# Pre-norm weights as columns at the eviction of transposed activations, in a two-layer encoder on one core

## The chip, the cores and the metric

The kernel runs on one core of a Trainium2 chip. The core has engines with instruction streams of their own: TensorE (PE in the profile, its weight loads PEld), VectorE (DVE), ScalarE (ACT), GpSimd (POOL) and SyncE (SP), which here issues nearly all DMAs. Data lies in SBUF on 128 partitions; TensorE writes to the 8 banks of PSUM. What counts is the time of one launch on the device in microseconds (us), lower being better.

## The reference

An encoder of two layers works on x of 256 tokens by 1024 channels in float32. Each layer is a block of three token mixers with gates and then an MLP, both with a norm ahead of them (pre) and one behind them (post):

```python
def rmsnorm(x, g):
    return x * lax.rsqrt(jnp.mean(x * x, axis=-1, keepdims=True) + EPS) * g

for l in range(2):
    h = rmsnorm(x, g_mix_pre[l])
    z = h @ w_in[l] + b_in[l]                     # 1024 -> 5648
    y_m = mlstm_branch(...) @ w_up_mlstm[l]       # convolution, two directions, chunks of 128
    y_f = fourier_branch(...) @ w_up_fourier[l]   # 2-D Fourier mixing
    y_s = s5_branch(...)                          # two-way diagonal state space, gelu, GLU
    gates = sigmoid(z[..., OFF_GATE:]).reshape(..., 3, 1024)
    mixed = gates[0] * y_m + gates[1] * y_f + gates[2] * y_s
    x = x + rmsnorm(mixed @ w_out[l], g_mix_post[l])
    h = rmsnorm(x, g_ffn_pre[l])
    f = square(relu(h @ w_ffn1[l])) @ w_ffn2[l]   # 1024 -> 4096 -> 1024
    x = x + rmsnorm(f, g_ffn_post[l])
```

## The kernel before

**Products.** Every large product is made of three of TensorE, in a type of fewer bits: high part by high part, high by low, low by high (`mm3`, L259). So each piece of weights (512 KB as a rule) comes by a DMA of SP into a raw buffer, ACT copies it to the high part (L200) and DVE subtracts that from it for the low part (L202, `wload`). There are three raw buffers and four of each part; some pieces take slots of the two rings A and B instead. The normalised activations lie transposed, channels on partitions, as a high and a low part, `hT`.

**Pre-norm** (`prenorm`, L349). It works on one half of the tokens, 128 rows, at a time. First, ACT squares and sums the rows in two halves of 512 channels (L353), and POOL makes a root column of the sums in two steps (L338, L340). Second, DVE multiplies each half by the root column and by the weight vector, which a DMA has broadcast to all partitions, in one instruction with two tensors (L359). Third, TensorE transposes four blocks of 128 channels of a half into one PSUM bank (L186); ACT evicts the bank into the high part (L368) with a constant factor and DVE makes the low part (L369). One instruction of each evicts 512 columns.

**Order.** A planner fixes the order of each engine's list ahead of the run. It takes what is emitted first, first, unless its own reckoning says that something later can go sooner; a load that waits for a buffer, for example, lets later loads pass. At the three joints, where one block's last products meet the next block's pre-norm and first weights, the order of ACT and DVE is written out by hand instead (`meet`, L395, with the strings of `MEET`, L58): `0` and `1` are the next stage of the norms of the first and second half of the tokens (`norms`, L371: squares of the sum, then its addition to x together with the squares of the pre-norm, then scaling, then transposes with their eviction), `h` and `l` are the high and low part of one of the next block's weights, `P` stands for the products of the second half.

**Weight vectors of the norms.** `load_gains` (L414) broadcasts the post-norm's and the next pre-norm's vector, 512 KB each, into one slot of ring A, with one weight load between them.

**Columns.** `load_columns` (L459) loads small vectors, among them biases, as 108 rows of 128, transposes them once and keeps them as columns, one element to a partition; `col` picks one.

**Start.** SP's list begins with a 128x128 unit matrix (the first columns of `cst`), three small loads of the S5 parameters (`s5_columns`, L493, some sixty small DVE instructions follow on them), the two halves of the first 128 rows of x, the broadcast pre-norm weights, the other 128 rows of x, and the first projection's weights: three pieces (gates of the mLSTM and Fourier input) and then four of v. Then come the rest of `cst`, eight loads of S5 tables with short rows (L586, L591), biases and columns. TensorE makes the first projections of the first half of the tokens and then of the second (`tokens`, L264).

Of the kernel before, what the change touches and what calls it, by code (L numbers as in the profile page):

```python
# [15 lines left out]
P = 128  # L16
D = 1024
# [31 lines left out]
# weights of the products that end a block held in place of the ring's pieces  # L49
TAIL = 4  # L50
# amount of work on the side for a pair of channel tiles: in the mixers of a layer, in its MLP from a pair on
# [3 lines left out]
# parts that the mLSTM with the Fourier mixing and the S5 have in that work  # L55
MIX_SHARE = ((2.0, 1.0), (1.0, 2.0))
# ends of the blocks: stages of the two norms (0, 1), of the next weights' high and low parts (h, l), the products (P)
# [23 lines left out]
def shape_constants():  # L81
# [16 lines left out]
    for g in range(2):  # L98
# [10 lines left out]
        ("bg", 16), ("s5d", 2)]  # L109
# [9 lines left out]
def encoder_kernel(ctx: ExitStack, tc: tile.TileContext, a: dict, out: bass.AP):  # L119
# [68 lines left out]
    def wload(pieces, shape, in_ring=None):  # L188
        """a piece of weights in two parts, in three stages: its loading, one of ACT and one of DVE"""
# [17 lines left out]
    def after_weights(l):  # L207
        """what DVE is to begin no sooner than the weights already asked for, in a later layer"""
        return tc.issue_after(latest[0]) if l > 0 else ExitStack()
# [4 lines left out]
    def now(gen):  # L214
        """all stages of gen; what it returns"""
        while True:
            try:
                next(gen)
            except StopIteration as e:
                return e.value  # L220

    class Feed:
        """the first weights of a block, stage by stage; each piece goes to the end of its list"""
# [40 lines left out]
    def tokens(t, parts, together):  # L264
        """rows t of the normalised activations times the weights of parts: what to do with the products, the number
        of columns, units, rows of tiles in a unit. The first half of the tokens comes when the weights do: the
        products that need their high parts alone go first"""
# [32 lines left out]
    def tick(budget):  # L300
        """let the work beside the main stream of products go on by about that amount"""
# [10 lines left out]
    def flush(which=None):  # L312
        """finish the work of one thread (or of both), the other going on beside it"""
# [7 lines left out]
    def wstat_pair(w, c0, nk, ahi, alo, kper=4, budget=0.0):  # L321
        """two [128 channels, 256 tokens] products of w[:, c0:c0+256]^T with the transposed activations, in one bank:
        its first product alone clears what the bank knows of what is written"""
# [11 lines left out]
    def rstd_of(ss):  # L335
        """(sum of squares / D + EPS)^-0.5 / sqrt(D) as a [128,1] column"""
# [12 lines left out]
    def prenorm(t, g):  # L349
        """rows t of x normalised, split and transposed into hT, in three stages"""  # L350
# [5 lines left out]
        hs = []  # L356
        for c in range(2):
            h = w2k()
            stt(h, x_sb[:, t, half(c)], rs, g[:, half(c)], ALU.mult, ALU.mult)  # L359
            hs.append(h)  # L360
        yield
        for c in range(2):
# [3 lines left out]
            o = [hT[i][:, c * 4:(c + 1) * 4, t * P:(t + 1) * P] for i in range(2)]  # L366
            p3 = ps.rearrange("p (k q) -> p k q", k=4)
            act(o[0], p3, AF.Copy, scale=ROOT_D)  # L368
            stt(o[1], p3, ROOT_D, o[0].bitcast(F32), ALU.mult, ALU.subtract)  # L369

    def norms(t, ps, gpost, gpre):  # L371
        """rows t of x take the sum of a block, normalised; then their normalisation for the next; four stages"""
# [18 lines left out]
    def ordered():  # L391
        """ACT and DVE take what is emitted here in this order"""
        return tc.manual_schedule(engines={mybir.EngineType.Activation, mybir.EngineType.DVE})

    def meet(products, chain0, chain1, feed, order):  # L395
        """the end of a block: the second half of the tokens' products beside the norms of the first half, the next
# [919 lines left out]
```

## Time and profile before

| what | value |
|---|---|
| three runs | 842.96, 845.17, 845.23 us; median 845.17 |
| span of the profiled execution, first to last instruction | 842.6 us |
| TensorE busy | 816.7 us (97%) |
| DVE busy | 605.7 us (72%) |
| ACT busy | 467.0 us (55%) |
| POOL busy | 29.3 us (3%) |
| moved by DMA | 146.32 MB, 174 GB/s on average |

The page gives no time of its own for the profiled execution beside the span, so the span is set against the three runs. A row of a timeline has the start in us from the span's start, the time in us from the group's first start to its last end, the engine, the line, the operation, what it writes and reads, how many instructions are merged in it, and in brackets how long the engine had been idle before and what ended that. Neighbouring instructions of one engine overlap a little, so the sum of durations can be more than the stretch that they fill.

### The profile page before, as it was taken

What the parts mean: (1) busy time and instruction counts of PE and PEld (TensorE: products, weight loads), DVE (VectorE), ACT (ScalarE), POOL (GpSimd) and SP (SyncE); (2) the same over time, 40 slices, a digit from 0 to 9 for tenths busy, and PEclk for the clock granted to TensorE, in tenths of its full rate; (3) what the DMA queues carried; (4) which work ended last, traced back from release to release, by engine and by line L of the source; (5) the groups of instructions that cost most, each with busy time, mean ns of one, the idle gap of its engine ahead of it and who ended that gap; (6) DMA issues with size and microseconds to landing.
All of it is one profiled execution on the core that took longest, in us unless ns stands there. A gap on an engine that the chain in (4) does not pass through costs nothing.

```text
span 842.6 us, 15382 instructions
## 1 busy us (share of the span) xinstructions
PE 816.7 (97%) x6077; PEld 757.2 (90%) x6077; DVE 605.7 (72%) x1087; ACT 467.0 (55%) x770; POOL 29.3 (3%) x50
## 2 busy tenths in 40 slices
PE   4999999999999999999989999999999999999997
PEld 3799999999878999999878999999997799999995
DVE  6798999787585576677477899787866845555554
ACT  4567844685464447567554444567655644444452
POOL 1000100010020000000010010000000100000000
PEclk9999999999999999999999999999999999999999
DMA  6775734446755665756656562454666556566571
GB/s 191 220 187 166 206 103 138 126 129 205 233 181 166 188 193 142 236 168 196 200 166 181 148 194 80 129 173 150 184 193 225 173 160 192 182 194 182 193 225 50
DMA packets 116965, 146.32 MB, mean 174 GB/s; under 512 B 17909, under 2 KB 98973, under 8 KB 116637
## 3 DMA queue, kind: packets, MB, share of 16 engines
q1 hardware_dynamic: 116892, 145.35, 57.7%
q8 instruction: 47, 0.77, 0.4%
q14 instruction: 26, 0.21, 0.1%
HBM read 143.80 MB, written 1.52 MB: 172 GB/s over the span
## 4 chain that ended last, share of the span: by engine, by line
PE 67%; issue 23%; DMA 4%; ACT 2%; DVE 2%; POOL 1%; SPq 1%; DVEq 0%; POOLq 0%; ACTq 0%
PE mm L260 14%; PE mm L261 14%; PE mm L262 14%; PE acc L261 4%; PE acc L260 4%; PE acc L262 4%; PE mm L277 2%; PE acc L735 2%; PE mm L276 2%; DMA raw<-in_w_ffn_dram 1%; PE acc L931 1%; PE acc L186 1%; DMA x_sb<-in_x_dram 1%; PE acc L914 1%; PE mm L293 1%
## 5 line engine op out<-in xcount | busy, mean ns | idle before, releaser
L202 DVE TENSOR_TENSOR wlo<-raw,whi 128x1024 fp32r<-128x1024 f32 (+1 forms) x237 | 287.6, 1215 | 170.8 <-ACT whi L200 170.1
L200 ACT ACTIVATE whi<-raw 128x1024 fp32r<-128x1024 f32 (+1 forms) x237 | 249.0, 1052 | 264.5 <-PE mm L261 136.8
L260 PE MATMUL mm<-hT,whi 128*128 128x256 f32 x1024 | 291.6, 285 | 0.0
L261 PE MATMUL mm<-hT,whi 128*128 128x256 f32 x1024 | 290.9, 284 | 0.0
L262 PE MATMUL mm<-hT,wlo 128*128 128x256 f32 x1024 | 290.1, 283 | 0.0
L260 PEld LDWEIGHTS mm<-hT,whi 128*128 128x128 f32 x1024 | 193.1, 189 | 1.6
L261 PEld LDWEIGHTS mm<-hT,whi 128*128 128x128 f32 x1024 | 192.6, 188 | 1.2
L262 PEld LDWEIGHTS mm<-hT,wlo 128*128 128x128 f32 x1024 | 193.4, 189 | 0.3
L261 PE MATMUL acc<-wlo,ringB 128*128 128x512 f32 x280 | 108.9, 392 | 0.8 <-DVE wlo L202 0.7
L262 PE MATMUL acc<-whi,ringB 128*128 128x512 f32 x280 | 108.4, 391 | 0.0
L260 PE MATMUL acc<-whi,ringB 128*128 128x512 f32 x280 | 105.6, 390 | 0.0
L261 PEld LDWEIGHTS acc<-wlo,ringB 128*128 128x128 f32 x280 | 52.6, 188 | 12.3 <-DVE wlo L202 2.0
L262 PEld LDWEIGHTS acc<-whi,ringB 128*128 128x128 f32 x280 | 52.6, 188 | 11.0
L260 PEld LDWEIGHTS acc<-whi,ringB 128*128 128x128 f32 x280 | 52.4, 188 | 10.2
L276 PE MATMUL mm<-whi,hT 128*128 128x512 f32 (+1 forms) x84 | 32.9, 394 | 3.1 <-ACT whi L200 2.8
L277 PE MATMUL mm<-whi,hT 128*128 128x512 f32 (+1 forms) x84 | 32.1, 385 | 1.9 <-DVE hT L369 1.8
L898 DVE SCALAR_TENSOR_TENSOR t1k<-ringB,pc,t1k 128x254 f32<-128x254 f32 (+1 forms) x64 | 31.4, 491 | 0.8
L262 PE MATMUL mm<-ringB,wlo 128*128 128x256 f32 x96 | 27.4, 286 | 0.0
L261 PE MATMUL mm<-ringB,whi 128*128 128x256 f32 x96 | 27.2, 283 | 0.0
L260 PE MATMUL mm<-ringB,whi 128*128 128x256 f32 x96 | 27.0, 283 | 0.0
L338 POOL TENSOR_SCALAR rs<-ss 128x1 f32<-128x1 f32 x16 | 7.1, 446 | 518.1 <-ACT t1k L376 320.3
L276 PEld LDWEIGHTS mm<-whi,hT 128*128 128x128 f32 x84 | 17.8, 213 | 7.2 <-ACT whi L200 3.8
(335 smaller groups left out, 1163.0 us busy)
## 6 DMA issues: line engine op xcount, KB each, us to landing
raw<-in_w_ffn_dram SPq DMA_DIRECT2D x128, 512.0 KB
raw<-in_w_in_dram SPq DMA_DIRECT2D x84, 512.0 KB
raw<-in_w_out_dram SPq DMA_DIRECT2D x16, 512.0 KB
raw<-in_w_glu_dram SPq DMA_DIRECT2D x16, 256.0 KB
raw<-in_w_up_mlstm_dram SPq DMA_DIRECT2D x8, 512.0 KB
ringB<-md SPq DMA_DIRECT2D x2, 1024.0 KB
raw<-in_w_up_fourier_dram SPq DMA_DIRECT2D x4, 512.0 KB
raw<-in_w_in_dram SPq DMA_DIRECT2D x4, 408.0 KB
```

Source lines behind the costliest of these rows:

```text
L186: nc.tensor.transpose(o, i, cst[:k, C_ID:C_ID + k])
L200: act(hi, raw, AF.Copy)
L202: latest[0] = V.tensor_sub(lo, raw, hi.bitcast(F32)).ins
L260: mm(o, lhi, rhi, start=start, stop=False)
L261: mm(o, lhi, rlo, start=False, stop=False)
L262: mm(o, llo, rhi, start=False, stop=stop)
L276: mm(o, hhi[:, k, tt], hi, start=k == 0, stop=False)
L277: mm(o, hlo[:, k, tt], hi, start=False, stop=False)
L293: mm(o, hhi[:, k, tt], units[k // kn][1][:, k % kn, :], start=False, stop=k == NK - 1)
L735: mm(bps[:, (g * 2 + r) * JN:(g * 2 + r + 1) * JN], QT[:, r, g0 + g, :], U[:, 4 * b + g, :], start=True, stop=True, skip_group_check=True)
L898: stt(u[:, lo_:hi_], z[:, lo_ + o:hi_ + o], col(l, "cw", j * 8 + i), u[:, lo_:hi_], ALU.mult, ALU.add)
L914: mm(sps[jt], qk[:, NH + h, jt * P:(jt + 1) * P], qk[:, h, :], start=True, stop=True, skip_group_check=True)
```

## The change

The pre-norm's weight vector is no longer multiplied in before the transposes but after them, where channels lie on partitions and the vector is a column. Scaling by the root is a `tensor_scalar` on DVE for the first half of the channels and an ACT copy with the root as its scale for the second. Each bank is evicted in four pieces of 128 columns, since each block of channels has a column of its own, by four ACT and four DVE instructions; the column holds the constant factor too. The columns of later pre-norms are 16 more rows in `load_columns`; the first one's come by a small load and a transpose of 8 rows of their own. `load_gains` broadcasts the post-norm's vector alone. At the start, x leads; its second half and the small load of weights are issued from ACT; two pieces of weights go ahead of the second rows of x; the S5 columns are emitted behind the pre-norms and the first weights. [...] Comments and docstrings fall away, which leaves the line numbers up to L349 as they were.

```diff
+        ("bg", 16), ("s5d", 2), ("gm", 8), ("gf", 8)]
...
     def prenorm(t, g):
...
-        hs = []
-        for c in range(2):
-            h = w2k()
-            stt(h, x_sb[:, t, half(c)], rs, g[:, half(c)], ALU.mult, ALU.mult)
-            hs.append(h)
+        hs = [w2k() for _ in range(2)]
+        V.tensor_scalar(hs[0], x_sb[:, t, half(0)], rs, None, ALU.mult)
+        act(hs[1], x_sb[:, t, half(1)], AF.Copy, scale=rs)
         yield
...
-            o = [hT[i][:, c * 4:(c + 1) * 4, t * P:(t + 1) * P] for i in range(2)]
-            p3 = ps.rearrange("p (k q) -> p k q", k=4)
-            act(o[0], p3, AF.Copy, scale=ROOT_D)
-            stt(o[1], p3, ROOT_D, o[0].bitcast(F32), ALU.mult, ALU.subtract)
+            for k in range(4):
+                o = [hT[i][:, c * 4 + k, t * P:(t + 1) * P] for i in range(2)]
+                gk = g[:, c * 4 + k:c * 4 + k + 1]
+                act(o[0], ps[:, k * P:(k + 1) * P], AF.Copy, scale=gk)
+                stt(o[1], ps[:, k * P:(k + 1) * P], gk, o[0].bitcast(F32), ALU.mult, ALU.subtract)
...
-    def load_gains(gpre, gpost, between=lambda: None):
-        gg = ring("A", [P, 2, D])
-        if gpost is not None:
-            nc.sync.dma_start(gg[:, 1, :], gpost.partition_broadcast(P))
+    def load_gains(gpost, between):
+        gg = ring("A", [P, D])
+        nc.sync.dma_start(gg, gpost.partition_broadcast(P))
         between()
-        if gpre is not None:
-            nc.sync.dma_start(gg[:, 0, :], gpre.partition_broadcast(P))
         return gg
...
+        put("gm", a["g_mix_pre"][l].rearrange("(r c) -> r c", c=P))
+        put("gf", a["g_ffn_pre"][l].rearrange("(r c) -> r c", c=P))
...
+        V.tensor_scalar(c[:, og:og + 16], c[:, og:og + 16], ROOT_D, None, ALU.mult)
...
-        gg = load_gains(a["g_ffn_pre"][l], a["g_mix_post"][l], after.load)
+        gg = load_gains(a["g_mix_post"][l], after.load)
+        gpre = col(l, "gf", 0, 8)
...
-        gg = load_gains(None if last else a["g_mix_pre"][l + 1], a["g_ffn_post"][l], after.load)
-        gpre = None if last else gg[:, 0]
+        gg = load_gains(a["g_ffn_post"][l], after.load)
+        gpre = None if last else col(l + 1, "gm", 0, 8)
...
+    nc.sync.dma_start(x_sb[:, 0, half(0)], a["x"][0, 0:P, half(0)])
+    nc.scalar.dma_start(x_sb[:, 0, half(1)], a["x"][0, 0:P, half(1)])
+    nc.sync.dma_start(cst[:, 0:P], a["cst"][:, 0:P])
+    grow = w2k()[0:8, 0:P]
+    nc.scalar.dma_start(grow, a["g_mix_pre"][0].rearrange("(r c) -> r c", c=P))
+    iu, vu, groups = [], [], []
+    feed = mixer_units(0, iu, vu)
+    for _ in range(2):
+        feed.load()
+    nc.sync.dma_start(x_sb[:, 1, :], a["x"][0, P:2 * P, :])
+    feed.load()
+    gps = mm_ps()
+    transpose(gps[:, 0:8], grow, 8)
+    g0 = per([P, 8], "g0")
+    V.tensor_scalar(g0, gps[:, 0:8], ROOT_D, None, ALU.mult)
+    for _ in prenorm(0, g0):
+        pass
+    for _ in prenorm(1, g0):
+        pass
+    feed.all()
     scols = s5_columns()
-    nc.sync.dma_start(cst[:, 0:P], a["cst"][:, 0:P])
     next(scols)
-    for c in range(2):
-        nc.sync.dma_start(x_sb[:, 0, half(c)], a["x"][0, 0:P, half(c)])
-    gg = load_gains(a["g_mix_pre"][0], None)
-    nc.sync.dma_start(x_sb[:, 1, :], a["x"][0, P:2 * P, :])
     tables = s5_tables(0)
     for _ in scols:
         pass
-    for _ in prenorm(0, gg[:, 0]):
-        pass
-    for _ in prenorm(1, gg[:, 0]):
-        pass
     side[1].append(tables)
-    iu, vu, groups = [], [], []
-    mixer_units(0, iu, vu).all()
```

## Rows read from the trace of the kernel before

**Rows 1.** Busy line of the page: us, share of the span, instructions.
```profile
PE 816.7 (97%) x6077; PEld 757.2 (90%) x6077; DVE 605.7 (72%) x1087; ACT 467.0 (55%) x770; POOL 29.3 (3%) x50
```

**Rows 2.** Stage table: stretch, length, busy us by engine, granted clock, DMA share, GB/s.
```profile
0.00:30.00 30.00, 15.93 (x83) 13.70 (x84) 19.32 (x63) 14.05 (x27) 2.15 (x10) 1.00 0.72 208
...
225.00:260.00 35.00, 33.30 (x163) 26.62 (x162) 25.72 (x32) 20.11 (x36) 4.50 (x8) 1.00 0.66 202
...
420.00:450.00 30.00, 27.00 (x136) 22.13 (x135) 21.80 (x32) 15.19 (x30) 3.76 (x8) 0.94 0.51 152
...
635.00:680.00 45.00, 44.05 (x227) 36.05 (x226) 30.35 (x37) 24.97 (x41) 4.60 (x8) 1.00 0.58 189
...
815.00:842.60 27.60, 21.46 (x115) 18.27 (x113) 11.54 (x14) 7.93 (x14) 1.72 (x4) 0.94 0.31 108
```

**Rows 3.** Timeline of SP's queue, 0 to 30 us.
```profile
0.72 0.39 SPq L1269 DMA_DIRECT2D cst<-in_cst_dram  x1
...
2.55 0.90 SPq L1272 DMA_DIRECT2D x_sb<-in_x_dram  x2
...
7.77 3.02 SPq L586 DMA_DIRECT2D ringB<-in_s_b_re_dram  x2
...
16.83 0.98 SPq L591 DMA_DIRECT2D ringB<-in_s_c_im_dram  x2
...
19.29 0.39 SPq L198 DMA_DIRECT2D raw<-in_w_in_dram  x1
```

**Rows 4.** Timeline of all engines, 0 to 20 us.
```profile
2.83 0.21 DVE L502 COPY Wt<-Wt 32x128 f32<-32x128 f32 x1 [2.83 <-DMA Wt<-in_s_log_dt_dram]
...
5.25 0.63 ACT L353 ACTIVATE t1k<-x_sb 128x512 bf16<-128x512 f32 x1 [3.25 <-DMA x_sb<-in_x_dram]
...
7.17 0.57 POOL L340 TENSOR_TENSOR rs<-rs,mhalf 128x1 f32<-128x1 f32 x1
...
10.65 1.41 DVE L359 SCALAR_TENSOR_TENSOR w2k<-x_sb,rs,ringA 128x512 f32<-128x512 f32 x2 [3.66 <-DMA ringA<-in_g_mix_pre_dram]
...
11.91 0.63 ACT L353 ACTIVATE t1k<-x_sb 128x512 bf16<-128x512 f32 x1 [5.27 <-DMA x_sb<-in_x_dram]
...
14.67 0.60 PE L276 MATMUL mm<-whi,hT 128*128 128x272 f32 x1 [1.24 <-ACT whi L200]
...
16.12 0.94 DVE L202 TENSOR_TENSOR wlo<-raw,whi 128x816 fp32r<-128x816 f32 x1
```

**Rows 5.** Timeline of ACT, 10 to 60 us.
```profile
24.81 1.06 ACT L200 ACTIVATE whi<-raw 128x1024 fp32r<-128x1024 f32 x1 [5.39 <-DMA raw<-in_w_in_dram]
```

**Rows 6.** Groups by line and shape: count, busy us, mean ns, idle before.
```profile
L359 DVE SCALAR_TENSOR_TENSOR w2k<-x_sb,rs,ringA 128x512 f32<-128x512 f32 x16 | 11.3, 747 | 8.9 <-POOL rs L340 5.2 <-DMA ringA<-in_g_mix_pre_dram 3.7
L369 DVE SCALAR_TENSOR_TENSOR hT<-acc,hT 128x512 fp32r<-128x512 f32 x16 | 10.4, 681 | 0.8 <-ACT hT L368 0.8
...
L368 ACT ACTIVATE hT<-acc 128x512 fp32r<-128x512 f32 x16 | 9.4, 594 | 6.7 <-PE acc L186 6.4
...
L894 DVE TENSOR_SCALAR t1k<-ringB,pc 128x256 f32<-128x256 f32 x16 | 6.4, 401 | 0.0
...
L939 ACT ACTIVATE t1k<-acc,rd 128x128 f32<-128x128 f32 x16 | 5.3, 365 | 5.0 <-DVE rd L937 5.0
L940 DVE SCALAR_TENSOR_TENSOR hm<-acc,rd,t1k 128x128 f32<-128x128 f32 x16 | 5.2, 345 | 1.6 <-ACT t1k L939 1.6
```

**Rows 7.** Timeline of TensorE at the first two joints.
```profile
240.31 1.32 PE L186 MATMUL acc<-cst,w2k 128*128 128x128 f32 x8 [0.75 <-DVE w2k L359]
...
434.55 1.32 PE L186 MATMUL acc<-cst,w2k 128*128 128x128 f32 x8 [1.87 <-DVE w2k L359]
```

**Rows 8.** Stretches of 0.5 us: TensorE busy, granted clock, DMA share, GB/s.
```profile
438.00:438.50 0.50, 0.50 (x4) 0.50 0.00 0
```

**Rows 9.** Stage table in steps of 10 us, columns as in the second group.
```profile
120.00:130.00 10.00, 10.00 (x87) 10.00 (x87) 10.00 (x30) 4.59 (x11) 0.00 (x0) 1.00 0.48 145
```

**Rows 10.** Timeline of ACT, 84 to 125 us.
```profile
105.76 1.55 ACT L1054 ACTIVATE ringA<-mm,pch 128x256 f32<-128x256 f32 x4
```

More of the change, by code (lines that the diff above doesn't have):

```diff
@@ L108 @@
 ROWS = [("s5b", 2), ("qkb", 8), ("ob", 4), ("gb", 24), ("cw", 40), ("cb", 8), ("ng", 4),
-        ("bg", 16), ("s5d", 2)]
+        ("bg", 16), ("s5d", 2), ("gm", 8), ("gf", 8)]
 ROFF = {}
@@ L483, in load_columns @@
         V.tensor_scalar(ch, c, 0.5, None, ALU.mult)
+        og = ROFF["gm"]
+        V.tensor_scalar(c[:, og:og + 16], c[:, og:og + 16], ROOT_D, None, ALU.mult)
         pc.append(c)
@@ L1163, in products @@
                         outproj(k, 1, [c])
-        meet(products, norms(0, aps[0], gg[:, 1], gg[:, 0]), norms(1, aps[1], gg[:, 1], gg[:, 0]), after, MEET[0][l])
+        meet(products, norms(0, aps[0], gg, gpre), norms(1, aps[1], gg, gpre), after, MEET[0][l])
     GROUPS = ((512, None), (256, "A"))
@@ L1264, in products @@
                         f2(kk, [1], [n], lead[-1])
-        meet(products, norms(0, aps[0], gg[:, 1], gpre), norms(1, aps[1], gg[:, 1], gpre), after, MEET[1])
+        meet(products, norms(0, aps[0], gg, gpre), norms(1, aps[1], gg, gpre), after, MEET[1])
+    nc.sync.dma_start(x_sb[:, 0, half(0)], a["x"][0, 0:P, half(0)])
[18 more added lines that the diff above has]
+    feed.all()
     scols = s5_columns()
-    nc.sync.dma_start(cst[:, 0:P], a["cst"][:, 0:P])
     next(scols)
-    for c in range(2):
-        nc.sync.dma_start(x_sb[:, 0, half(c)], a["x"][0, 0:P, half(c)])
-    gg = load_gains(a["g_mix_pre"][0], None)
-    nc.sync.dma_start(x_sb[:, 1, :], a["x"][0, P:2 * P, :])
     tables = s5_tables(0)
@@ L1302 @@
     from concourse.bass_utils import run_bass_kernel_spmd as _run
-    nc = _bacc.Bacc("TRN2", target_bir_lowering=False, num_devices=1)
+    nc = _bacc.Bacc("TRN2", target_bir_lowering=False, num_devices=1,
+                     dynamic_dma_scratch_size=1024)
     arrays, aps = {}, {}
```

## The prediction

> **What bounds the kernel now.** I read the busy line of the page first: TensorE is busy 816.7 of 842.6 us [rows 1], so all that a change can give back is 25.9 us of its idle time, unless TensorE's work itself gets shorter or its clock higher. Then I asked the stage table where these 25.9 us lie [rows 2]: 14.07 before 30 us, 1.70 at the end of the first mixer (225 to 260), 3.00 at the end of the first MLP (420 to 450), 0.95 at the end of the second mixer (635 to 680) and 6.14 behind the last products (815 on). These five make 25.86, so every other stretch is full. The last one is the final post-norm and the stores, where no pre-norm follows and the diff changes only the shape of a weight tile; I give it nothing. The change can therefore earn at most 19.7 us, 14.1 of them at the start.
>
> The start I read in order of time [rows 3, 4]. The first half of x is issued behind four smaller loads at 2.55 and its squares begin at 5.25; the root is there at 7.74 (7.17 + 0.57); but the scaling starts only at 10.65, and its row names the broadcast weight vector as what it waited for (3.66). The first product of the first projection follows at 14.67. The second rows of x are seen at 11.91. After those projections TensorE wants the first piece of v's weights: SP issues it at 19.29, and ACT converts it at 24.81 after 5.39 of waiting for it [rows 3, 5]. SP could not issue it sooner for two reasons: its buffer comes free when DVE has split the first piece (16.12 + 0.94 = 17.06) [rows 4], and SP is held from 7.77 to 17.81 by the eight S5 table loads (four rows of two each, of which the first and the last stand in [rows 3]), 1.25 us for each against 0.45 for a half of x.
>
> **The change part by part.** (1) The first pre-norm. x's first half moves from 2.55 to the head of SP's queue at about 0.72, the place of the first issue now, so 1.83 sooner; the other half goes to ACT's queue. Squares and root keep their length (5.25 to 7.74), so the root comes at about 5.9. The broadcast is gone, and with it the 3.66 [rows 4]: scaling at 5.95 rather than 10.65, 4.7 sooner. The new 8-row transpose and its tiny DVE step for the weight column lie in the wait for the root; if their 4 KB load came late, they would cost their lateness, but it is issued in ACT's queue as its second.
>
> (2) Scaling. Now two DVE instructions of 0.747, one behind the other [rows 6]. Then DVE does one half without a tensor of weights and ACT the other. No row shows either. For DVE the nearest are a tensor_scalar on half as many columns with two column operands, 0.401, and today's 0.747; I take 0.5, nearer the first, which is the same operation. For ACT I take 0.65, between the 0.594 of a 512-column eviction with a constant scale and 0.747. Both halves are done after 0.65 rather than 1.41 (the pair overlaps a little [rows 4]), the first after 0.5 rather than 0.75.
>
> (3) Eviction. Now ACT 0.594 and DVE 0.681 for each half [rows 6]; then four pieces each of 128 columns with a column scale. The cell evictions are the same two operations on the same shape: ACT 0.365, DVE 0.345. Four make 1.46 and 1.38, so ACT spends 0.87 more a half, 14 us over the kernel, and DVE 0.70 more, less the 0.25 to 0.75 that scaling saves on it; both lie beside TensorE's work everywhere but at the joints. At a joint the first product pair needs one piece of each, 0.71, where it needed 1.28 now: 0.57 sooner. The last piece of a half comes later by up to 0.5, but TensorE takes one piece per two products, and all 8 pieces of ACT cost 2.9 at most against 3.7 of products with 512 columns.
> [...]
>
> (4) SP's queue at the start. The broadcast's issue and one half of x leave it, two issues of 0.45 to 0.47. The three S5 column loads move behind the first projection's weights and still stand before the table loads, so they change nothing for v. 512 KB leave the DMA engines: at the stretch's 208 GB/s [rows 2] that is 2.5 us. So the table loads are through and v's first piece is issued about 3.4 sooner, if only this counts. The lower end is 1.0, the issue time alone, if the table loads are slow by themselves and not because the engines are full. The upper end: the buffer comes free with the first pre-norm, which is 4.7 to 6.7 sooner, and if SP's list then puts v ahead of the table loads, they no longer matter. But TensorE has its work before v: from the scaling at 10.65 to 24.81 are 14.2 us, of which the first product's wait for a conversion, 1.24 [rows 4], and some 0.75 of scaling and eviction can go. From 5.95 on that makes 18.1, so v can be wanted 6.7 sooner at most. Between 1.0 and 6.7 I take 4.5: the 3.4 that the rows give, and one more for a list that will be partly reordered in v's favour, since the buffer comes free well before the table loads have ended.
>
> (5) The S5 column chain goes behind all this: some sixty DVE instructions of 0.2, begun at 2.83 now [rows 4], will begin near 10. Nothing reads them before the S5 tables. DVE is free for 10.7 of the first 30 us [rows 2], which hides it; without that cover it would cost up to 7 at the tables (a rival below).
>
> (6) The joints. First mixer: TensorE waits 0.75 for the scaling [rows 7], and again for the first low part. 0.25 of (2) and 0.57 of (3) come off: 0.7 of the 1.70, as DVE has a weight split between the two. First MLP: it waits 1.87 for the scaling [rows 7]. Here ACT's list, written by hand, puts its half of the scaling ahead of the other rows' squares, which now run while ACT has nothing else, and these ahead of the evictions; that costs 0.3 to 0.65 on ACT, against 0.25 and 0.57 won and 0.4 by the faster pair: 0.8 of the 3.00. Second mixer: 0.7 of 0.95. Together 2.2. The ends: 5.65 if all idle time goes, and a loss of 1.0 if the small evictions pace the products. [...]
>
> (7) Four broadcasts of 512 KB become 16 more rows in the loads of small columns, two small issues a layer, 0.3 each, and one tiny DVE multiplication: nothing on the path, TensorE being full there.
>
> **Sum.** 4.5 + 2.2, less 0.1 for the new small work: 6.6. The profiled span of 842.6 becomes 836.0. The three times are 842.96, 845.17 and 845.23, so the median lies 2.6 over that span and the lowest run 0.4; taken from the median the time is 838.5.
>
> **The rivals.** The forecast as above, 838.5: 0.50.
> - v's first piece stays behind the table loads. For it: SP's 1.25 per load, and the whole list before v is kept. Against: the engines are full just then and lose 512 KB. Start 1.0, joints 2.2, so 3.1: 842.1. Chance 0.18.
> - v overtakes the table loads, start 6.7, joints 2.2, and the clock stays up, 1.5: 10.4, 834.8. For it: the buffer is free at about 11. Against: the list is fixed ahead by a planner that I can't see. Chance 0.20.
> - The small evictions bound the joints: of the 14 us that ACT gains by (3), a third of a us lands on TensorE at each joint instead of the 0.7 won, so 4.5 - 1.0 = 3.5, 841.7. For it: ACT's list is fixed there by hand. Against: 2.9 of ACT under 3.7 of products. Chance 0.06. [...]
> - Slower: the S5 tables of the first layer come too late. DVE has nothing left from 120 to 130 (10.00 of 10.00) [rows 9], and at 105.76 ACT evicts two finished banks of gates in one go, behind the tables' last eviction, whose buffer they take [rows 10]. With four banks TensorE can run about two more pairs of products, some 11 us, before it stops. If the column chain starts 7 late and DVE never catches up, while TensorE comes 4.5 sooner, it just stops; to be slower than now by 2.5 the tables must be over 13 late. It decides from there, microsecond for microsecond: 848. Against: DVE's 10.7 idle at the start. Chance 0.06.
>
> **How the numbers follow.** A measurement of this kernel tells about 0.3%, 2.5 us, from no change: the bound is 842.6. Forecast and overtaking are under it almost entirely, the first rival in half of its cases, the small evictions in most: 0.83 faster. Slower only by the last: 0.06. The rest, 0.11, within. The range goes from 832.5 (some 12.4 us: both best ends) to 843.0 (2.2 us: joints only) and leaves out the slow rival and the ends.
>
> **What would show it.** Scaling before 7 us with no wait for weights, and the first product near 8: step 1. SP's issue of v's first piece near 15 and its conversion near 20: step 4; near 18 and 24 is the first rival, near 11 the second. ACT's pieces at about 0.37, DVE's at 0.35: step 3. Idle time of TensorE before 30 us at 9 to 10 rather than 14.1, at the joints 0.2 to 2.2 each. Any idle time of TensorE near 105 or in 30 to 200 would be the slow rival, and the prediction wrong.

## The result, and the profile after

Four runs of the changed kernel took 863.84 to 865.71 us, median 865.32; the kernel before took 842.96 to 845.77 beside it. The ratio is 1.0252, 95% interval 1.0233 to 1.0271: slower by 2.5%, where 838.5 was forecast. The profiled span is 863.8 us.

The page of the changed kernel, busy line and granted clock in 40 slices:

```profile
PE 828.6 (96%) x6078; PEld 758.8 (88%) x6078; DVE 608.1 (70%) x1130; ACT 484.6 (56%) x826; POOL 33.2 (4%) x50
...
PEclk9999999989999999999989999999999999999999
```

The stage table of the changed kernel, columns as in [rows 2]:

```profile
0.00:30.00 30.00, 21.33 (x107) 18.36 (x108) 17.85 (x64) 20.11 (x42) 2.07 (x10) 1.00 0.80 246
150.00:170.00 20.00, 16.36 (x166) 15.67 (x166) 15.14 (x37) 8.16 (x19) 0.00 (x0) 0.91 0.28 80
180.00:200.00 20.00, 16.50 (x112) 14.66 (x111) 12.55 (x27) 10.69 (x22) 3.04 (x2) 0.83 0.35 106
225.00:260.00 35.00, 32.06 (x152) 25.00 (x152) 22.38 (x32) 20.42 (x39) 4.79 (x8) 1.00 0.55 169
260.00:300.00 40.00, 36.81 (x212) 31.05 (x210) 20.46 (x28) 18.75 (x28) 0.00 (x0) 0.96 0.53 162
420.00:450.00 30.00, 29.04 (x149) 23.99 (x148) 17.55 (x26) 14.99 (x31) 2.58 (x6) 0.96 0.56 178
635.00:680.00 45.00, 42.93 (x229) 35.20 (x228) 29.59 (x39) 25.95 (x47) 4.79 (x8) 0.99 0.57 177
```

In the first row TensorE is busy for 21.33 us where [rows 2] have 15.93: the start won 5.4. The two rows between 150 and 200 are new: 3.6 and 3.5 us without a product in a first mixer that had been full, and a lowered clock behind each (0.91 and 0.83). TensorE's waits there are for the last step of the S5 branch's gelu (L784) and for the mLSTM norm (L956); a line gives the waiting instruction, what ended the wait, the us in total, how often, and the longest:

```profile
PE acc L790 <- DVE w2k L784: 3.6, 1, 3.6
PE acc L186 <- ACT hm L956: 3.5, 1, 3.5
```

Behind the first joint, 260 to 300 us, 3.2 us are empty and the clock is down again (0.96).

The start of the changed kernel, timeline of all engines:

```profile
4.44 0.63 ACT L353 ACTIVATE t1k<-x_sb 128x512 bf16<-128x512 f32 x1 [1.39 <-DMA x_sb<-in_x_dram]
...
6.86 0.72 ACT L358 ACTIVATE w2k<-x_sb,rs 128x512 f32<-128x512 f32 x1
6.86 0.48 DVE L357 TENSOR_SCALAR w2k<-x_sb,rs 128x512 f32<-128x512 f32 x1 [1.39 <-POOL rs L340]
...
9.02 0.57 PE L276 MATMUL mm<-whi,hT 128*128 128x272 f32 x1
9.03 0.37 SPq L198 DMA_DIRECT2D raw<-in_w_in_dram  x1
...
13.23 1.06 ACT L200 ACTIVATE whi<-raw 128x1024 fp32r<-128x1024 f32 x1
```

Scaling, first product, the issue of v's first piece and its conversion come 3.8, 5.65, 10.3 and 11.6 us sooner than in [rows 3], [rows 4] and [rows 5].

The first joint of the changed kernel, timeline of ACT, DVE and TensorE:

```profile
244.50 0.37 ACT L367 ACTIVATE hT<-acc,pc 128x128 fp32r<-128x128 f32 x1 [0.78 <-PE acc L186]
244.90 0.35 DVE L368 SCALAR_TENSOR_TENSOR hT<-acc,pc,hT 128x128 fp32r<-128x128 f32 x1 [0.28 <-ACT hT L367]
...
245.28 0.37 ACT L367 ACTIVATE hT<-acc,pc 128x128 fp32r<-128x128 f32 x1 [0.42 <-DVE hT L368]
...
245.69 0.35 DVE L368 SCALAR_TENSOR_TENSOR hT<-acc,pc,hT 128x128 fp32r<-128x128 f32 x1 [0.43 <-ACT hT L367]
...
249.88 0.35 DVE L368 SCALAR_TENSOR_TENSOR hT<-acc,pc,hT 128x128 fp32r<-128x128 f32 x1 [0.44 <-ACT hT L367]
...
250.84 0.50 PE L276 MATMUL mm<-whi,hT 128*128 128x512 f32 x1 [1.63 <-ACT whi L200]
```

The brackets tell it: ACT waits 0.42 for DVE's piece and DVE 0.43 for ACT's, in turn, so within a bank a pair of pieces costs 0.78 us, and the eight fill 244.50 to 250.23. ACT is held until 249.84, and the next weights, queued behind the pieces on ACT, are late: TensorE waits 1.63 for their conversion. The same over all three joints, from the groups of the changed kernel (48 pieces, busy us, mean ns, idle time before them and what ended it):

```profile
L367 ACT ACTIVATE hT<-acc,pc 128x128 fp32r<-128x128 f32 x48 | 16.9, 365 | 18.1 <-DVE hT L368 15.0 <-PE acc L186 3.2
```

Of ACT's 18.1 us of idle time between these pieces 15.0 are waits for DVE. In [rows 6] ACT's 512-column evictions have 6.7, of which TensorE ends 6.4.

To see where the time goes, the kernels are cut at the roots of the norms on POOL (L338), which mark the two chains of each joint: "J" is from the first root of the first chain to the last of the second.

| kernel | to the 1st joint | J1 | to the 2nd | J2 | to the 3rd | J3 | to the last norm |
|---|---|---|---|---|---|---|---|
| before | 234.99 | 13.22 | 181.17 | 10.35 | 206.10 | 13.24 | 171.64 |
| after | 238.62 | 16.80 | 183.93 | 14.25 | 206.15 | 16.67 | 175.40 |
| four then four | 235.88 | 13.73 | 177.98 | 11.51 | 203.24 | 13.74 | 169.97 |
| joints shifted | 231.18 | 13.72 | 178.40 | 11.51 | 203.24 | 13.72 | 170.18 |
| before shifted | 231.18 | 13.16 | 180.02 | 10.54 | 203.03 | 12.92 | 169.88 |

The last three are experiments told below. After against before: 3.6 lost by the first joint although the start won 5.4, 10.9 in the three joints and 6.6 in the stretches behind them.

### The profile page after: what moved, and what is told of

Its sections match the earlier page's. It is cut to its first block, busy times and chain, and to the rows that moved or that the text cites. A ratio compares the mean times of both kernels' runs of the same rounds, so it can differ in the third digit from the quotient of the medians.

```text
span 863.8 us, 15499 instructions
## 1 busy us (share of the span) xinstructions
PE 828.6 (96%) x6078; PEld 758.8 (88%) x6078; DVE 608.1 (70%) x1130; ACT 484.6 (56%) x826; POOL 33.2 (4%) x50
## 4 chain that ended last, share of the span: by engine, by line
PE 68%; issue 23%; ACT 3%; DVE 3%; POOL 1%; DMA 1%; SPq 0%; POOLq 0%; DVEq 0%; ACTq 0%
PE mm L260 13%; PE mm L261 13%; PE mm L262 13%; PE acc L260 5%; PE acc L261 5%; PE acc L262 5%; PE acc L186 2%; PE acc L735 2%; PE mm L277 2%; PE mm L276 2%; PE acc L931 1%; DVE hT L368 1%; ACT hT L367 1%; PE acc L771 1%; PE acc L774 1%
## 5 line engine op out<-in xcount | busy, mean ns | idle before, releaser
L260 PE MATMUL acc<-whi,ringB 128*128 128x512 f32 x280 | 107.7, 393 | 3.2 <-ACT whi L200 3.2
L262 PE MATMUL acc<-whi,ringB 128*128 128x512 f32 x280 | 108.6, 391 | 0.0
L276 PE MATMUL mm<-whi,hT 128*128 128x512 f32 (+1 forms) x84 | 35.6, 432 | 4.1 <-ACT whi L200 2.2
L277 PE MATMUL mm<-whi,hT 128*128 128x512 f32 (+1 forms) x84 | 35.7, 430 | 2.5 <-DVE hT L368 2.5
L276 PEld LDWEIGHTS mm<-whi,hT 128*128 128x128 f32 x84 | 17.6, 213 | 11.6 <-ACT hT L367 6.3
L338 POOL TENSOR_SCALAR rs<-ss 128x1 f32<-128x1 f32 x16 | 7.5, 468 | 525.7 <-ACT t1k L375 324.8
```

Of the source, the lines that this page charges most:

```text
L260: mm(o, lhi, rhi, start=start, stop=False)
L262: mm(o, llo, rhi, start=False, stop=stop)
L276: mm(o, hhi[:, k, tt], hi, start=k == 0, stop=False)
L277: mm(o, hlo[:, k, tt], hi, start=False, stop=False)
```

## The experiments

"Step" is the mean distance of the starts of neighbouring products with 256 columns (all pairs under 200 ns apart, some 3480 in each trace); the ratio is to the kernel before.

| run | us | ratio (95%) | step, ns | first joint at |
|---|---|---|---|---|
| before | 843 to 845 | | 119.7 | 234.99 |
| after | 865.32 | 1.0252 (1.0233 to 1.0271) | 117.6 | 238.62 |
| e1 four then four | 838.58 | 0.9931 (0.9905 to 0.9956) | 117.4 | 235.88 |
| e2 banks in turn | 849.93 | 1.0069 (1.0046 to 1.0092) | 117.6 | 237.47 |
| e3 S5 columns early | 860.87 | 1.0202 (1.0181 to 1.0223) | 117.4 | 236.49 |
| e4 e2 and e3 | 848.44 | 1.0054 (1.0034 to 1.0075) | 117.4 | 236.57 |
| e5 start alone | 851.92 | 1.0094 (1.0059 to 1.0129) | 119.6 | 241.22 |
| e6 joints alone | 844.39 | 0.9999 (0.9985 to 1.0013) | 119.7 | 233.68 |
| e7 e1 and S5 early | 842.59 | 0.9975 (0.9963 to 0.9986) | 117.5 | 237.48 |
| e8 e1, fewer taps | 837.55 | 0.9911 (0.9888 to 0.9934) | 117.4 | 233.30 |
| e9 before shifted | 834.64 | 0.9906 (0.9885 to 0.9927) | 117.3 | 231.18 |
| e10 e1, no shift | 847.78 | 1.0059 (1.0037 to 1.0080) | 119.7 | 236.71 |
| e11 e6 shifted | 836.24 | 0.9920 (0.9906 to 0.9935) | 117.5 | 231.18 |
| e12 e7, share 2.8 | 838.91 | 0.9953 (0.9938 to 0.9968) | 117.6 | 234.70 |
| f1 activations shifted | 843.24 | 0.9982 (0.9965 to 0.9999) | 119.6 | 233.27 |
| f3 e7, share 2.5 | 838.85 | 0.9939 (0.9920 to 0.9958) | 117.5 | 234.20 |
| f4 start, S5 early, shifted | 845.53 | 1.0016 (0.9991 to 1.0040) | 117.4 | 239.85 |
| f5 f4, share 2.5 | 839.03 | 0.9937 (0.9912 to 0.9961) | 117.5 | 233.31 |
| f6 both beside | 835.19 | 0.9907 (0.9882 to 0.9932) | 117.4 | 231.41 |
| f7 shifted behind activations | 834.75 | 0.9896 (0.9879 to 0.9912) | 117.3 | 230.52 |

### The order of the pieces (e1, e2)

e1, on the changed kernel:

```diff
             for k in range(4):
                 ...
                 act(o[0], ps[:, k * P:(k + 1) * P], AF.Copy, scale=gk)
-                stt(o[1], ps[:, k * P:(k + 1) * P], gk, o[0].bitcast(F32), ALU.mult, ALU.subtract)
+            for k in range(4):
+                ...
+                stt(o[1], ps[:, k * P:(k + 1) * P], gk, o[0].bitcast(F32), ALU.mult, ALU.subtract)
```

> The changed kernel, with one edit in the pre-norm: of each bank of four transposed blocks, ACT's four pieces are emitted first and DVE's four behind them, where the two were emitted in turn. Theory (one bank, one reader at a time): in the changed kernel each pair of pieces of a bank costs 0.78 us (0.37 of ACT, then 0.41 of DVE, one waiting for the other), 6.3 for the eight pairs of 128 tokens. With four and four, DVE takes bank 0 while ACT takes bank 1: 3 x 1.45 = 4.4. Each of the six pre-norms at the joints ends 1.9 sooner; the one that starts a block counts fully, the second in part: 1.9 to 3.8 a joint, 6 to 11 in all, 854 to 859 us from 865.3. Rival A (the small pieces are slow by their fixed cost, or the order by hand of ACT's list is what delays): the pieces keep their pace, 865. Rival B (the joints don't count, all of the loss is in the first mixer): pieces faster, time 865.

e2 has both banks transposed first, then the pieces with `for k in range(4): for c in range(2):`.

> The changed kernel, with one edit in the pre-norm: both banks of transposed blocks are written first, then the pieces are evicted in turn from bank 0 and bank 1, ACT and DVE each on the bank that the other has just left. Theory (one bank, one reader at a time): now 8 pieces of ACT at 0.37 run while DVE runs beside them, 3.4 us for 128 tokens where the changed kernel has 6.3; the first product pair waits for four transposes more, some 0.7. The joints win back 2.2 to 2.9 for the first tokens and up to as much for the second: 7 to 14 in all, 851 to 858 us, and a little better than four then four. Rival A (fixed cost or order by hand): 865. If the theory holds for the joints alone, the waits of TensorE in the first mixer at 150 to 200 us stay.

The first joint of e1, timeline of ACT and DVE, and its row of the stage table behind that joint:

```profile
241.76 2.18 ACT L371 ACTIVATE hT<-acc,pc 128x128 fp32r<-128x128 f32 x8 [0.77 <-PE acc L186]
...
242.93 2.17 DVE L374 SCALAR_TENSOR_TENSOR hT<-acc,pc,hT 128x128 fp32r<-128x128 f32 x8 [1.05 <-ACT hT L371]
...
243.77 1.11 ACT L200 ACTIVATE whi<-raw 128x1024 fp32r<-128x1024 f32 x1
...
260.00:300.00 40.00, 39.68 (x259) 35.78 (x259) 23.10 (x29) 18.03 (x22) 0.00 (x0) 1.00 0.64 195
```

The same sixteen instructions now fill 241.76 to 245.10, 3.3 us where they took 5.7, and DVE begins as soon as ACT has left the first bank. Nothing interrupts either engine within its eight pieces any more, and a piece in a run of eight costs 0.27 us where one alone took 0.37. ACT goes on to the next weights at 243.77, and behind the joint TensorE is full at full clock. Over the three joints ACT's waits for DVE are gone:

```profile
L371 ACT ACTIVATE hT<-acc,pc 128x128 fp32r<-128x128 f32 x48 | 13.1, 391 | 1.9 <-PE acc L186 1.9
```

What ACT waited for isn't the tile `hT`, which DVE reads: in e1 ACT writes pieces of it while DVE reads others. The wait stands in the built program, by bank: in the changed kernel and in e2 ACT's second to fourth piece of a bank at the joints each carry a wait for DVE's piece before in that bank, in e1 none does. Both expectations underrated it: e1 gains 26.7 us on the changed kernel instead of 6 to 11, e2 15.4 instead of 7 to 14. By the table, of e1's gain 8.7 lie in the joints, 14.3 in the stretches behind them, 2.7 in the first mixer. So it is shown that the alternation, and not the number of small pieces, makes the changed kernel slow. e2 stays behind e1, contrary to what was expected: with those waits its eight pieces fill 3.16 us on ACT rather than 2.18, and the weights' conversions wait for that. How far this makes up the whole difference isn't shown: of the 8.4 us between the two profiled spans 2.2 lie in the joints.

### The first mixer (e3, e4, e5, e7, e8, e12, f3 to f5)

e3, on the changed kernel, brings the S5 columns back ahead of the pre-norms; e4 is e2 and e3; e7 is e1 and e3:

```diff
     nc.sync.dma_start(x_sb[:, 1, :], a["x"][0, P:2 * P, :])
+    scols = s5_columns()
+    next(scols)
     feed.load()
+    tables = s5_tables(0)
+    for _ in scols:
+        pass
...
     feed.all()
-    scols = s5_columns()
-    next(scols)
-    tables = s5_tables(0)
-    for _ in scols:
-        pass
```

> The changed kernel, with the S5 column work (three loads and some sixty small DVE steps) moved back ahead of the first two pre-norms in the program's text; x, the constants and the first two pieces of weights are still issued ahead of its loads. Theory (the late S5 chain starves the first mixer): the changed kernel loses 9 us between 150 and 200 us, where TensorE waits for the last steps of the S5 branch and of the mLSTM norm, because DVE's S5 work runs 7 to 18 us late from 20 us on. With it early again the first mixer has no such waits and the chains at the first joint start some 5 sooner than in the kernel before: 865.3 - 9 = 856, joints unchanged. Rival (the mixer's loss comes from elsewhere: the alternating evictions, the earlier TensorE, ACT's list): 863 to 866, with the waits at 150 to 200 us still there. If the early S5 steps hold up the first scaling, the start loses up to 5 of its gain: 858 to 861.

> The changed kernel with both edits: S5 columns early, and the two banks evicted in turn. If the two causes are separate and make up the loss, the gains add: 7 to 14 from the joints and 9 from the first mixer, 842 to 849, near the kernel before (845.2) or a little under it. If they are one cause (DVE's lost time at the joints and in the mixer), the sum is less than its parts: 851 to 856. If neither holds: 865.

e3 gained 4.5 us, not 9, and the joint came 2.1 sooner, not 9. The two waits were gone, but one of 6.1 us for the mLSTM norm stood between 180 and 190, with the clock at 0.83 over 180 to 210. e4 gave 1.5 on e2, with intervals that overlap. That the late S5 columns are the whole cause fell.

e5 is the kernel before with the diff's start alone, its first pre-norm included:

> The kernel before with the new start alone: x first, small weight column, first pre-norm with the scaling split and 128-column evictions, S5 columns behind it. All other pre-norms are as before (broadcast weights, 512-column evictions). Theory M1: the first mixer ends on its side work on DVE and ACT, so TensorE's 4 to 5 us of lead are lost in waits between 100 and 200 us, whatever happens at the joints: the first chain of the first joint starts at 234 to 239 us (234.99 in the kernel before) and the time is 843 to 849. Theory M2 (the mixer's loss belongs to the small evictions, through the planner's lists): no waits there, first chain at 230, 840. The forecast's own step for the start alone was 4.5: 840.7.

Stages of e5:

```profile
0.00:30.00 30.00, 21.53 (x109) 18.32 (x110) 18.37 (x70) 20.24 (x43) 2.08 (x10) 1.00 0.84 246
150.00:180.00 30.00, 26.36 (x251) 25.65 (x250) 23.77 (x55) 16.60 (x39) 0.00 (x0) 0.94 0.30 82
180.00:210.00 30.00, 26.51 (x191) 24.67 (x191) 21.27 (x36) 17.19 (x33) 3.05 (x2) 0.89 0.42 129
```

The start wins 5.6 (21.53 against 15.93), the mixer then loses 7.1 to waits, and the lowered clock costs some 5 more by an estimate: if it is 0.50 while it is lowered, as in [rows 8], then 0.94 and 0.89 over 30 us each are 3.6 and 6.6 us at half speed, half of which is lost. The joint comes 6.2 later and the time is 8.1 up, 2 to 3 past what M1 had allowed. The step that was forecast to earn 4.5 us loses 8 by itself.

> Four then four, with the S5 columns early as well. In the pair with the two banks in turn the early columns gave 1.5 us (849.9 to 848.4) and moved the mixer's wait from the S5 branch to the mLSTM norm. The same here: 837, with a wait of TensorE of some 6 us for the norm between 180 and 190. If the two waits had separate causes, and the reordered lists happen to serve both, up to 5 more: 833.

e7 came out at 842.6, slower than e1, and missed. TensorE's wait in its first mixer, and DVE's timeline ahead of it:

```profile
PE acc L186 <- ACT hm L962: 6.0, 1, 6.0
...
169.77 0.68 DVE L1118 SCALAR_TENSOR_TENSOR w2k<-w2k,w2k 128x512 f32<-128x512 f32 x1
...
173.17 0.69 DVE L1118 SCALAR_TENSOR_TENSOR w2k<-w2k,w2k 128x512 f32<-128x512 f32 x1
...
176.18 0.69 DVE L1118 SCALAR_TENSOR_TENSOR w2k<-w2k,w2k 128x512 f32<-128x512 f32 x1
...
179.51 0.67 DVE L1118 SCALAR_TENSOR_TENSOR w2k<-w2k,w2k 128x512 f32<-128x512 f32 x1
180.10 0.34 DVE L946 SCALAR_TENSOR_TENSOR hm<-acc,rd,t1k 128x128 f32<-128x128 f32 x1
...
182.26 0.35 DVE L946 SCALAR_TENSOR_TENSOR hm<-acc,rd,t1k 128x128 f32<-128x128 f32 x1
...
187.58 0.17 DVE L958 SCALAR_TENSOR_TENSOR nb<-mv,rsd 128x8 f32<-128x8 f32 x1 [2.06 <-POOL rsd L956]
```

The gates' combining steps (L1118 to L1120), ready sooner since TensorE is ahead, stand in front of the last two cells (L946) for which TensorE then stops. In DVE's list four rounds of them have begun (L1118) ahead of the norm (L958); in the kernel before it is one. Two ways to tell order from amount:

```diff
-        for j in (0, 1, 3, 4):
+        for j in ((1, 3) if l == 0 else (0, 1, 3, 4)):
```

> Four then four, where the first layer's convolution leaves out the outer two of its five taps: 16 DVE instructions of 0.40, 6.4 us of DVE work fewer in the first mixer (the output is that of a three-tap convolution in that layer). Theory M1, in the form that DVE's work in the first mixer is the bound: the waits of 3.4 and 1.2 us go or shrink to under 1, the first joint's chain starts 4 to 6 sooner (230 to 232 rather than 235.9), 833 to 835. Rival M3 (it is the order that the planner gives the side work, not its amount; or a latency chain from the S5 tables over the scans to the gelu): a wait of 3 us or more stays somewhere between 100 and 200, 837 to 839.

```diff
-MIX_TICK = (2.3, 2.5)
+MIX_TICK = (2.8, 2.5)
```

> Four then four with the S5 columns early, and the share of side work that is taken up with each pair of products in the first layer's mixer raised from 2.3 to 2.8. In the list of the kernel without this, DVE has four of the gates' combining steps ahead of the last mLSTM cells, and TensorE waits 6.0 us for the mLSTM norm; with 2.8 one such step stands ahead, as in the kernel before. Theory M3 (the lead is lost to the order that the lists give the side work): the wait of 6.0 is gone or under 1.5, the clock stays at full speed behind it, the first joint's chain starts at 230 to 232 (237.5 without), 833 to 836. Theory M1 (DVE's amount of work bounds the first mixer): a wait of 4 us or more appears at another place, 839 to 843.

e8 gained 1.0 us, no more than a measurement tells, and its first joint came 2.6 sooner where 4 to 6 were expected; its waits were 5.7 us in three places, and DVE was idle for 10.6 us of 90 to 120. So the amount of DVE's work alone isn't the bound. e12 moved the norm forward as wanted and gained 3.7 on e7 by the medians (1.9 by the ratios, whose intervals just overlap); its wait of 2.7 us appeared at the S5 tables, at 69 us, with the clock at 0.89 over 60 to 90. Order matters, but neither theory had it right. The last three tried a share between the two, and the new start beside the old joints at the better place of the tiles:

> Four then four, S5 columns early, the share of side work 2.5, between 2.3 (wait of 6.0 us for the mLSTM norm, 842.6) and 2.8 (2.7 us for the S5 tables, 838.9). If it is the order alone (M3), a share between them can serve both: waits under 1.5 in all, 833 to 836, first joint's chain at 231 to 233. If the amount of work that has to be done by a point bounds it (M1): 838 to 842, with one of the two waits, or parts of both.

> The kernel before with the 32 bytes (834.6) and the new start, with the S5 columns ahead of the first pre-norms; all other pre-norms as before. M1 and M3 both let the mixer wait some 6 us for the mLSTM norm, as in the two runs with early columns: 837 to 841, first joint's chain at 233 to 237 (231.2 without the new start). If the new start's lead is kept here: 829 to 831, chain at 226.

> The same with the share of side work at 2.5. M3: the waits go, 829 to 832, the best of all runs. M1: 834 to 839, with waits of 3 to 6 us in the first mixer.

f3's waits, as in e12, sit at the tables:

```profile
PE acc L186 <- ACT QT L676: 2.7, 1, 2.7
```

f3 came out where M1 has it. f4 waited 6.1 us for the norm and 1.1 for the tables and is 10.9 above e9 by the medians (9 by the ratios), 4.5 over the top of what was expected; f5 waited 3.2 in three places and is 4.4 above e9 (2.6 by the ratios), the upper end of M1. In none of the thirteen kernels with the new start (the changed one and twelve experiments) is the first joint reached sooner than with the old start and the same step (231.2 in e9 and e11 with the short one; 233.7 in e6 and 235.0 before with the long one). It is shown that the lead is used up in the first mixer under every order tried. Whether an order exists that keeps it, or the chain of the S5 tables over DVE, ACT and POOL forbids it, stays open.

### The place of the tiles (e6, e9 to e11, f1, f6, f7)

e6 has the old start and e1's joints:

> The old start (S5 columns first, broadcast weights and DVE's two scalings for the first pre-norm) with the new joints in their better order: weight columns at the eviction, ACT's four pieces of a bank, then DVE's four; scaling split over both engines. If the start is worth nothing in the end (M1) and the joints are worth the 5.5 us that the run with four then four shows between the first joint and the end, then 839 to 840 and the first joint's chain at 235.0 as before. If the start's lead is partly kept in that run, 841 to 843. The forecast's step for the joints was 2.2: 843.

It came out at 844.4, above all that was expected, although its joints are those of e1. The segments tell why: e1's stretches of full TensorE are shorter (177.98 and 203.24) than those of the kernel before (181.17 and 206.10), and e6's are not (180.48 and 205.73). TensorE's work itself had become quicker. The largest groups of products, before and then e9:

```profile
L260 PE MATMUL mm<-hT,whi 128*128 128x256 f32 x1024 | 291.6, 285 | 0.0
L261 PE MATMUL mm<-hT,whi 128*128 128x256 f32 x1024 | 290.9, 284 | 0.0
L262 PE MATMUL mm<-hT,wlo 128*128 128x256 f32 x1024 | 290.1, 283 | 0.0
```

```profile
L260 PE MATMUL mm<-hT,whi 128*128 128x256 f32 x1024 | 289.1, 282 | 0.0
L261 PE MATMUL mm<-hT,whi 128*128 128x256 f32 x1024 | 287.4, 281 | 0.0
L262 PE MATMUL mm<-hT,wlo 128*128 128x256 f32 x1024 | 287.0, 280 | 0.0
```

The diff's `g0`, eight columns of 4 bytes, stands ahead of all buffers of weights on each partition and moves them by 32 bytes. Before, they begin 32 bytes beside a multiple of 64 and the activations at one; after, both begin at one (by the addresses in the built programs: the first buffer of high parts at 125408 before and 110336 after, `hT` at 29760 and 14400). e9 does that to the kernel before, and apart from it only takes the changed kernel's build parameter `dynamic_dma_scratch_size=1024`, the smaller DMA scratch, with which the first tile begins at 1152 rather than 16512, both multiples of 64; e10 takes it from e1; e11 gives it to e6:

```diff
     oth = per([P, NH, S], "oth")
+    per([P, 8], "unused")
```

> The kernel before with an unused column of 32 bytes on each partition (and the smaller DMA scratch of the changed kernel, which makes room for it). All tiles of weights, raw, high and low parts, rings and working tiles, then begin 32 bytes further on: at a multiple of 64, as in the changed kernel, where the kernel before has them 32 bytes beside one. Nothing else changes. Theory P (place): in the three runs so far whose tiles lie as before (before, the start alone, the joints alone), neighbouring products with 256 columns start 119.7 ns apart; in the seven whose tiles lie as after, 117.5; 3484 such steps, 7.6 us. So 835.5 to 838.5 here, with steps of 117.5 and no other difference. Rival (the step comes from the columns' code, the order of the lists or the data): 843 to 846, 119.7.

> The run with four then four, with the eight-column tile of the first weight vector put into a tile that is not used yet, so that the weights' tiles lie as in the kernel before. Theory P: steps of 119.7 ns and 838.6 + 7.6 = 844 to 847: the new start and the reordered columns together are then worth nothing, and the whole gain of that run is the place of the tiles. Rival (the gain is that of start and joints, as the forecast had it): 837 to 840.

> The joints alone (old start, four then four) with the unused 32 bytes. Theory P: 844.4 - 7.6 = 836 to 838, and still no waits of TensorE in the first mixer, unless a TensorE that is 2.6 us quicker there runs into the late side work too (then 838 to 840). Rival: 844.

All three came within 1 us of the range that the theory of the place has: 834.6, 847.8, 836.2, with steps of 117.3, 119.7 and 117.5; the rival is out in each. The steps account for 2.3 ns x 3480 = 8 us. The smaller DMA scratch isn't the cause, since e6, e10 and f1 have it and the long step. f1 puts the 32 bytes ahead of `hT` instead; f6 has one such tile ahead of `hT` and one behind `oth`; f7 has one right behind `hT`:

> As the kernel before with 32 unused bytes, but these lie ahead of the transposed activations: now the activations (the moving operand of the 256-column products, the stationary one of the 512-column ones) begin 32 bytes beside a multiple of 64, and the weights, the rings and all that follows at a multiple of 64. If the stationary operand's place sets the step: 117.5 ns and 834 to 836, as with the bytes behind the activations; the products of 128 tokens with 512 columns, whose stationary operand is now beside a multiple, may take a little longer (some 100 of them). If the moving operand's place sets it: 119.7 or more, 842 to 845.

> As the kernel before with two unused columns of 32 bytes, one ahead of the transposed activations and one behind the last lasting tile: activations and weights both begin 32 bytes beside a multiple of 64. If the two operands want the same place within 64 bytes: steps of 117.5 ns, 834 to 837. If each wants a multiple of 64: 119.7 or more, 842 to 847.

> As the kernel before with the 32 unused bytes right behind the transposed activations, so that activations, S5 tables, the gated outputs and the weights all begin at a multiple of 64. In the run with the bytes behind the last lasting tile the 180 products of the S5's gated outputs went from 119 to 121 ns, since these outputs stayed beside a multiple while the weights moved. Here they keep 119: some 0.4 us under that run, 833.5 to 835.5, the best of all runs if anything tells them apart.

f1 lost the gain (119.6), f6 had it (117.4) with both operands 32 bytes beside a multiple. So it is neither operand's own place: of the two places tried, 0 and 32 bytes beside a multiple of 64, the two want the same. In e9 the mean step of the S5's gated outputs is only 1.2 ns longer than in f7, 0.2 us for 180 products and not the 0.4 expected, and f7 can't be told from e9 by its time; both are the best of all runs, and they beat the kernel before by 0.9 to 1.0% and the changed one by 3.4%.

## Why the prediction was wrong

The ratio comes apart in three factors, since e1 and e10 each undo one thing: the alternating pieces (after against e1) 1.032, or 26.7 us; the place of the tiles (e1 against e10) 0.987, 9 to 11 us gained; start and columns in the better order (e10 against before) 1.006, some 4 to 5 us lost. By the steps of the prediction:

1. First pre-norm: 4.7 sooner forecast, 3.8 measured. The wait for weights is gone as forecast; but the first half of x, issued 1.83 sooner, was there only 0.81 sooner (4.44 against 5.25), so it took 3.7 us from its issue where it had taken 2.7.
2. Scaling: 0.5 and 0.65 forecast, 0.48 and 0.72 measured. Right.
3. Eviction: **the step that failed.** The durations were right (0.37 and 0.35), the rate was not. "All 8 pieces of ACT cost 2.9 at most against 3.7 of products" let ACT run through; it took 5.3, since it waited for DVE within each bank. The rows of the kernel before show only half of such a turn: in [rows 6] DVE's 512 columns wait for ACT's, which they read. That ACT would wait for DVE before the next piece of a bank no row there shows, since ACT evicts a bank at one go. The trace after shows it: 0.42 and 0.43 of waiting in turn in one bank, and 15.0 us of such waits on ACT over the three joints; in e1, where the two work on different banks, none. The size of the pieces was the lesser matter: in e1's run of eight a piece costs 0.27, where the prediction took 0.365.
4. v's weights: 4.5 forecast; SP's list put the first piece behind two of the eight table loads and ahead of the other six (9.03), nearly the overtaking rival's case, and TensorE's idle time before 30 us fell by 5.4. The 1.5 that this rival has for a clock that stays up no run shows: over 420 to 450 us the clock was 0.94 before and 0.96 after, and e6, where it was 1.00, took the time of the kernel before (0.9999). The size of 4.5 was right, the gain didn't last: the rows of a full TensorE between 30 and 225 us don't say that what feeds it could have gone faster.
5. S5 columns, costed at nothing under DVE's idle time at the start: wrong. The rival "slower" had named this chain, but 105 us as its place and 0.06 as its chance. The waits began at 157 and 186 us (3.6 and 3.5). That this chain alone makes them isn't shown: with the columns early (e3) both are gone, but 6.1 us of waiting for the norm come in their place. Each of the two waits was also followed by a lowered clock (0.91 and 0.83 in the rows), which no term of mine had for a new stall.
6. Joints: 2.2 forecast. In the better order they give nothing that can be measured: 0.9999 in e6, and e11 against e9 0.9920 to 0.9906, intervals that overlap. J1 to J3 are longer by 0.6 to 1.0 each than in e9. As the diff has them, they are most of the loss. The rival on small evictions had the place right and priced it at 1.0.
7. Broadcasts into columns, "nothing": right for the work (e6), but `g0`, the small tile of the first weights, moved every weight by 32 bytes, which gained more than the whole sum of the forecast. The prediction had set aside the case that "TensorE's work itself gets shorter"; e9 shows that it did.

That four then four ran at 838.6, the forecast time, is luck: its gain is the 32 bytes, not the start and joints that were to earn it. The last sentence of the prediction holds: idle time of TensorE between 30 and 200 us showed it wrong.

## What to carry to other kernels

When one eviction is cut into pieces for two engines, count the turns within a PSUM bank, not the pieces: let one engine finish a bank and go to the next before the other begins (0.78 us for a pair of pieces in turn here, 0.27 for a piece in a run). A gain at the start of a full engine is a gain only if what feeds it later has room to follow (here 5.4 us were won before 30 us, and the first joint came 3.6 later), so look for who is nearly full behind it. And before an edit is credited with one per cent, compare the steps of untouched products (119.7 and 117.4 ns here): a tile of 32 bytes can move every operand behind it.

## What the runs showed of the hardware

A 256-column product with 128x128 weights starts on the mean some 117.4 ns after its neighbour when activations and weights begin at the same place within 64 bytes, and 119.7 when they lie 32 bytes apart (means of 117.3 to 117.6 and 119.6 to 119.7 in all twenty traces). Not every step grows: of the steps between products of `hT` with weights 44 to 45% take 121 ns or more in the five traces with the long mean, and under 1% in the other fifteen.

The same direction holds for two smaller groups, all means of steps under 200 ns: the products of the S5's gated outputs start 118.7 ns apart when they lie as their weights do (before, f1, f7) and 119.9 when not (e9, f6); the first projections with 256 columns 114.4 to 114.9 when alike (e9, f6, f7) and 118.2 to 119.1 when not (f1, before). Products of the mLSTM's up-projection had 119.6 to 120.0 in all five of these kernels, though their operands always lay alike, so this is not the whole rule. Products with 512 columns keep their 227 ns (median). Why the place matters, no run here shows.

The changed kernel's mean granted clock is 0.982, where the kernel before has 0.996. The clock records of the two traces hold 1.00 and 0.50 alone. At 0.50 are some 31 us of the changed kernel, from 160.7, 188.0, 273.3, 447.4, 679.5 and 860.4 us on, against 7 before, from 436.5 and 839.3 on. The first two stretches follow the two waits in the first mixer; but in e2, whose wait for the gelu is as long (3.6), the clock is 1.00 over 150 to 180, so what length of wait lowers it isn't shown. In those stretches of the changed kernel neighbouring products with 256 columns start 213 ns apart (median of 20 pairs) where 117.6 is the mean of all, so where TensorE is full nearly half of that time is lost, beside the waits themselves.
